# Batched matmul on one core: the first loads take their runs in another order over the partitions

One Trainium2 chip, one core. The metric is the time of one execution on the device in microseconds, as the median of several runs.

## The reference

```python
def setup_inputs():
    batch, m, k, n = 16, 512, 512, 512
    # a: [batch, k, m] float32, b: [batch, k, n] float32, normal random numbers

def reference(a, b):
    return np.matmul(a.transpose(0, 2, 1), b).astype(np.float32)
```

Sixteen products of 512 x 512 matrices. A and B are 16.8 MB each, the output is 16.8 MB: 50.33 MB go through the DMA engines, as q1 counts them.

## The kernel before

The first two batches are loaded one by one, with four rows of 512 numbers (8 KB) per partition, so that the first matmuls can start when one batch of A and B has landed. All later batches are loaded in pairs, with 16 KB per partition. Which row of k sits in which partition doesn't matter to the result, as long as A and B agree, because the contraction sums over all of them.

```python
P = 128; RV = 4; R = 8                      # the program derives these
# run p (rows 4p .. 4p+3, 8 KB) goes to partition p
in0_v = [x.rearrange("batch (p r) m -> batch p r m", r=RV) for x in (a, b)]
...
for j in range(2):                          # j = 0 is A, j = 1 is B
    nc.sync.dma_start(x_ts[j][:, 0:RV, :], in0_v[j][0]).then_inc(s_f[j], 16)    # batch 0
for j in range(2):
    nc.sync.dma_start(x_ts[j][:, RV:R, :], in0_v[j][1]).then_inc(s_x[j], 16)    # batch 1
for n in range(2, 2 * pairs):               # pairs of batches, 2 MB each
    if n >= NX:
        nc.sync.wait_ge(s_in, n - NX + 1)   # until a buffer has been cast
    ...
# VectorE casts a landed tile to bf16, TensorE multiplies, ScalarE copies PSUM out;
# SP issues seven outputs once the last input's first half is in, and the eighth at the end
```

Of the kernel before, what the change touches and what calls it, by code (L numbers as in the profile page):

```python
# [8 lines left out]
def kernel(  # L9
# [6 lines left out]
    nc = tc.nc  # L16
    P = 128
    batch, K, M = a.shape
# [9 lines left out]
    R = K // Q  # L28
    V = 2
    RV = R // V  # L30
# [3 lines left out]
    in_v = [x.rearrange("(pair g) (q r) m -> pair (g q) r m", g=G, r=R) for x in (a, b)]  # L34


    in0_v = [x.rearrange("batch (p r) m -> batch p r m", r=RV) for x in (a, b)]
    out_v = out.rearrange("(pair g) (c t) n -> pair c g t n", g=G, t=T)

    NX = 4  # L40
# [10 lines left out]
    x_ts = [pool.tile([P, R, M], f32, name=f"x{j}") for j in range(NX)]  # L51
# [5 lines left out]
    s_x = [tc.alloc_semaphore(f"s_x{j}") for j in range(NX)]  # L57
    s_f = [tc.alloc_semaphore(f"s_f{j}") for j in range(2)]
# [9 lines left out]

    with tc.tile_critical(no_gpsimd_drain=True):  # L69
        for j in range(2):  # L70
            nc.sync.dma_start(x_ts[j][:, 0:RV, :], in0_v[j][0]).then_inc(s_f[j], 16)
        for j in range(2):
            nc.sync.dma_start(x_ts[j][:, RV:R, :], in0_v[j][1]).then_inc(s_x[j], 16)
        for n in range(2, 2 * pairs):
            if n >= NX:
                nc.sync.wait_ge(s_in, n - NX + 1)
            src, x = in_v[n % 2][n // 2], x_ts[n % NX]
# [141 lines left out]
```

## Time and profile before

| | before |
|---|---|
| time, median of the first 3 runs | 123.24 us (123.08 to 123.38) |
| span of the profiled run | 121.7 us |
| DMA engines' share of the span | 97.8% |
| busiest compute engine | TensorE, 53% |
| first DMA issued, first packet, first cast | 0.94 us, 1.96 us, 5.81 us |

The table of stretches that the prediction shows says the rest: half rate for the first 1.3 us of transfers, then a steady 430 GB/s to the end.

### The profile page before, as it was taken

How to read it: one execution, taken by the hardware profiler on the slowest of the kernel's cores; microseconds unless marked ns; L12 is line 12 of the kernel's file. 1: busy time of each engine (PE TensorE's matmuls, PEld its weight loads, DVE VectorE, ACT ScalarE, POOL GpSimd, SP SyncE). 2: the span in 40 equal slices, each digit the busy share in tenths (PEclk: the TensorE clock that was granted, in tenths of full speed). 3: DMA queues.
4: the chain of work that ended last, by engine and by line, in shares of the span. 5: the costliest groups of instructions: out<-in, count | busy, mean ns of one | idle time of the engine just before them, and what ended most of it. 6: DMA issues, size and time to landing. Idle time of an engine off the chain costs nothing. (4 is left out here: it accounts for less than half of the span.)

```text
span 121.7 us, 1207 instructions
## 1 busy us (share of the span) xinstructions
PE 65.0 (53%) x480; PEld 35.6 (29%) x480; DVE 38.0 (31%) x48; ACT 32.2 (26%) x41; POOL 0.2 (0%) x4
## 2 busy tenths in 40 slices
PE   0007937919989759739969919999930000000000
PEld 0002302306646336414536605556610000000000
DVE  0051061095684094082464446266000000000000
ACT  4000330330390840840191480065190000000000
POOL 0000000000000000000000000000000000000000
PEclk9999996799999999976999996899999555555555
DMA  3999999999999999999999999999999999999993
GB/s 59 428 428 426 463 431 431 431 431 436 431 431 431 431 431 431 431 431 431 431 431 431 431 431 399 431 420 423 426 428 423 428 431 431 431 431 428 431 428 162
DMA packets 4912, 50.33 MB, mean 414 GB/s; under 512 B 432, under 2 KB 432, under 8 KB 432
## 3 DMA queue, kind: packets, MB, share of 16 engines
q1 hardware_dynamic: 4912, 50.33, 97.8%
HBM read 33.55 MB, written 16.78 MB: 414 GB/s over the span
## 5 line engine op out<-in xcount | busy, mean ns | idle before, releaser
L151 PE MATMUL ps<-bbf,abf 64*128 64x512 bf16 x448 | 53.1, 394 | 11.9 <-PEq L146 11.9
L151 PEld LDWEIGHTS ps<-bbf,abf 64*128 64x128 bf16 x448 | 31.4, 113 | 33.7 <-issue 19.2
L176 ACT COPY o<-ps 128x1024 f32<-128x1024 f32 x28 | 26.3, 1026 | 39.3 <-PE ps L151 39.3
L113 DVE CAST abf<-x 128x2048 bf16<-128x2048 f32 x14 | 17.2, 1225 | 20.6 <-PE ps L151 14.9
L113 DVE CAST bbf<-x 128x2048 bf16<-128x2048 f32 x14 | 17.1, 1224 | 11.8 <-DMA x<-in_b_dram 11.8
L131 PE MATMUL ps<-bbf,abf 128*128 128x512 bf16 x32 | 11.9, 554 | 12.5 <-PEq L129 12.5
L131 PEld LDWEIGHTS ps<-bbf,abf 128*128 128x128 bf16 x32 | 4.3, 138 | 19.6 <-issue 19.1
L170 ACT COPY o<-ps 128x1024 f32<-128x1024 f32 x4 | 4.1, 1014 | 19.2 <-PE ps L131 19.2
L94 DVE CAST abf<-x 128x2048 bf16<-128x2048 f32 x2 | 2.5, 1228 | 12.7 <-PE ps L131 6.9
L94 DVE CAST bbf<-x 128x2048 bf16<-128x2048 f32 x2 | 2.5, 1226 | 1.2 <-DMA x<-in_b_dram 1.2
L181 ACT ACTIVATE done<-done 1x1 uint32<-1x1 uint32 x8 | 1.6, 197 | 0.0
L170 ACT ACT_TABLE_LOAD x1 | 1.3, 1283 | 0.9 <-SPq L69 0.9
L119 DVE MEMSET done<- 1x1 f32 x14 | 0.8, 59 | 0.0
L98 DVE MEMSET done<- 1x1 f32 x2 | 0.1, 59 | 0.0
L203 POOL MEMSET const-uint8-127<- 128x1 uint8 x1 | 0.1, 103 | 0.0
L203 POOL MEMSET const-bfloat16-1.0<- 128x1 bf16 x1 | 0.1, 102 | 0.0
L203 POOL MEMSET const-float32-0.0<- 128x1 f32 x1 | 0.1, 99 | 0.2 <-issue 0.2
L203 POOL MEMSET const-float32-1.0<- 128x1 f32 x1 | 0.1, 99 | 0.0
## 6 DMA issues: line engine op xcount, KB each, us to landing
out_dram<-o SPq DMA_DIRECT2D x8, 2048.0 KB, 22.2
x<-in_a_dram SPq DMA_DIRECT2D x7, 2048.0 KB, 12.1
x<-in_b_dram SPq DMA_DIRECT2D x6, 2048.0 KB, 15.6
x<-in_b_dram SPq DMA_DIRECT2D x4, 1024.0 KB, 12.1
x<-in_a_dram SPq DMA_DIRECT2D x2, 1024.0 KB, 6.8
```

The lines of the kernel that those rows point to most:

```text
L94: nc.vector.tensor_copy(out=bf_ts[0][:], in_=x_ts[j][:, u * RV:(u + 1) * RV, :]).then_inc(s_cast, 1)
L98: nc.vector.memset(dve_done[:, j:j + 1], 0.0).then_inc(s_in, 1)
L113: nc.vector.tensor_copy(out=(bbf_ts if n % 2 else abf_ts)[v][:], in_=x_ts[n % NX][:, v * RV:(v + 1) * RV, :],).then_inc(s_cast, 1)
L119: nc.vector.memset(dve_done[:, n:n + 1], 0.0).then_inc(s_in, 1)
L131: mm = nc.tensor.matmul(ps_ts[0][h][:, t % 2, :], a_m[:, r, t], bbf_ts[0][:, r, :], start=(r == 0), stop=(r == RV - 1),)
L151: mm = nc.tensor.matmul(ps_ts[g][h][:, t % 2, :], a_m[:, t], bbf_ts[v][rows, r, :], start=(v == 0 and r == 0), stop=(v == V - 1 and r == R ...
L170: nc.scalar.copy(out=o_ts[0][:, g, 2 * h:2 * h + 2, :], in_=ps_ts[0][h][:]).then_inc(s_ev[h], 1)
L176: ev = nc.scalar.copy(out=o_ts[i % NO][:, g, 2 * h:2 * h + 2, :], in_=ps_ts[g][h][:])
L181: nc.scalar.memzero(act_done[:, i:i + 1]).then_inc(s_out, 1)
L203: nc = _bacc.Bacc("TRN2", target_bir_lowering=False, num_devices=1)
```

## The change

Its intent: partitions 0, 4, 8 and so on are to read neighbouring 8 KB runs of DRAM rather than runs 32 KB apart. Partition 4s+i now takes run 32i+s, for A and B alike. "Starts" are below the first addresses that partitions 4s ask for: 32 KB apart before, 8 KB apart after, and 64 KB apart in the later loads of 16 KB per partition. "Hops" are the distances from one partition to the next within such a group of four: 8 KB before, 256 KB after. Both are read from the program.

```diff
-    in0_v = [x.rearrange("batch (p r) m -> batch p r m", r=RV) for x in (a, b)]
+    in0_v = [x.rearrange("batch (i s r) m -> batch s i (r m)", i=4, r=RV) for x in (a, b)]
...
-            nc.sync.dma_start(x_ts[j][:, 0:RV, :], in0_v[j][0]).then_inc(s_f[j], 16)
+            nc.sync.dma_start(x_ts[j][:, 0:RV, :].rearrange("p r m -> p (r m)"), in0_v[j][0]).then_inc(s_f[j], 16)
...
-            nc.sync.dma_start(x_ts[j][:, RV:R, :], in0_v[j][1]).then_inc(s_x[j], 16)
+            nc.sync.dma_start(x_ts[j][:, RV:R, :].rearrange("p r m -> p (r m)"), in0_v[j][1]).then_inc(s_x[j], 16)
```

The source has three dimensions now (32, 4, 2048).

## The prediction

No trace shows which engine takes which run, and a rival rested on it, in which the first 4 MB would take up to twice as long (an assumption: 133 us, chance 0.03; that was the whole chance given to slower by over 2%). The sum: +0.02 us for the issue, -0.25 us for the first packet and 0 for the rest, in all -0.23 us, so 123.0 us. The 9.8 us in the rival on hops is 4.19 MB at the 430 GB/s of the stretches.

> **What bounds the kernel now.** I read the page's summary first, then its DMA rows, then the chain of waits, then a table of stretches of time that I cut by hand, and last the single DMA packets of the trace.
>
> ```profile
> span 121.7 us, 1207 instructions
> PE 65.0 (53%) x480; PEld 35.6 (29%) x480; DVE 38.0 (31%) x48; ACT 32.2 (26%) x41; POOL 0.2 (0%) x4
> DMA  3999999999999999999999999999999999999993
> GB/s 59 428 428 426 463 431 431 431 431 436 431 431 431 431 431 431 431 431 431 431 431 431 431 431 399 431 420 423 426 428 423 428 431 431 431 431 428 431 428 162
> q1 hardware_dynamic: 4912, 50.33, 97.8%
> ```
>
> No compute engine is busy for more than 53% of the span; the 16 DMA engines are busy for 97.8% of it, and the bytes per slice stand at about 430 GB/s from the second slice to the last but one. So the span is 50.33 MB at that rate (50.33 MB / 430 GB/s = 117.0 us) plus what happens before the stream is at its rate and after its last byte: 121.7 - 117.0 = 4.7 us. Only the first slice is weak (59 GB/s), and the last (162 GB/s). The chain of waits agrees in its own way: it holds compute of a total of 8% of the span and ends when the eighth output was issued at 91.7 us; everything after that is data draining.
>
> The next table cuts the span where the single packets change their behaviour. The last three columns are the granted TensorE clock, the DMA engines' mean busy share and what they moved.
>
> ```profile
> 0.00:1.95 1.95, 0.00 (x0) 0.00 (x0) 0.00 (x0) 1.05 (x1) 0.20 (x4) 1.00 0.00 0
> 1.95:3.25 1.30, 0.00 (x0) 0.00 (x0) 0.00 (x0) 0.23 (x1) 0.00 (x0) 1.00 1.05 214
> 3.25:4.25 1.00, 0.00 (x0) 0.00 (x0) 0.00 (x0) 0.00 (x0) 0.00 (x0) 1.00 1.02 426
> 4.25:18.45 14.20, 6.57 (x16) 2.26 (x16) 4.51 (x5) 2.03 (x2) 0.00 (x0) 1.00 1.01 430
> 18.45:64.20 45.75, 36.24 (x281) 20.15 (x283) 22.90 (x31) 17.27 (x23) 0.00 (x0) 0.93 1.01 432
> 64.20:91.60 27.40, 22.21 (x186) 13.22 (x182) 10.57 (x14) 11.58 (x17) 0.00 (x0) 0.94 1.00 426
> 91.60:119.40 27.80, 0.00 (x0) 0.00 (x0) 0.00 (x0) 0.00 (x0) 0.00 (x0) 0.55 1.01 427
> ```
>
> Three things are to be seen. Nothing moves for 1.95 us: launch, and the first DMA's issue. Then for 1.30 us the engines count as fully busy and yet move 214 GB/s, half the rate. From 3.25 us on the rate is 426 to 432 GB/s whatever is moved: the two first batches in 8 KB runs (to 18.45 us), later inputs in 16 KB runs, outputs in 8 KB runs.
>
> The packets explain the 1.30 us. The median 8 KB packet takes 309 ns (8192 B / 309 ns x 16 = 424 GB/s), the 16 KB one 611 ns. The first packet of each of the 16 streams is different. Eight streams start at 1.96 to 2.04 us and their first packet takes 1.12 to 1.29 us; the other eight start at 2.12 to 2.21 us and take 0.79 to 0.87 us. Every second packet is back at 309 ns. The 16 KB loads and the later 8 KB packets show nothing of the kind, except for one or two packets per stream at 314 to 328 ns near 4.1 us. I chained the packets to streams by their ends (the trace doesn't name the engine). A stream's time over 309 ns per packet is 0.87 to 1.0 us in the slow eight and 0.50 to 0.57 us in the fast eight, nearly all of it the first packet; one stream also loses 0.25 us to slightly slow packets at 84 to 90 us, and it ends last, at 120.34 us. The streams have no gaps, so what is lost at the start is still there at the end: the slow eight end at 120.0 to 120.1 us, the fast at 119.75 to 119.9 us.
>
> [...]
>
> **The change part by part.** It removes no byte, no DMA, no wait and no instruction. The four DMAs of 1 MB each keep 128 runs of 8 KB and their destination. Only which run goes where moves: partition 4s+i gets run 32i+s. A and B change alike, so the contraction, which sums over all 128 partitions, is the same sum in another order: casts (1.23 us each, 4 in this part) and matmuls (32 of them) cost the same. In order of time:
> 1. Issue. The first DMA's issue takes 392 ns, the second 422 ns, with the plain two-dimensional source; a later partial load, whose source is strided, takes 433 ns. A third source dimension may cost a like amount: an estimate of 0 to 0.04 us on the path for the first DMA, nothing for the other three, which are issued while data flows.
> 2. First packet. [...] If all of the first packet's excess came from the spread of the starts, the slow eight would gain 1.23 - 0.31 = 0.92 us. If the slow eight merely came to the 0.80 us of the fast eight, they would gain about 0.4 us, and the stream that ends last, one of the slow eight at its start, would end at about 119.9 us. If the excess is just the wait for the first data of an idle memory system, nothing is gained. I take 0.92 us at a chance of 0.1, 0.4 us at 0.4, nothing at 0.5: 0.25 us.
> 3. The rest of the 4 MB. [...] The streams are held at 309 ns by something that 64 KB starts, 32 KB starts, reads and writes share, so I expect no loss: 0 us.
> 4. From there on all is shifted. Compute has slack: the first cast starts when A has landed (5.81 us), and DMA issues that wait for a cast are ahead of need, as the missing gaps show. A gain at the start should arrive whole at the end.
> Sum: +0.02 - 0.25 = -0.23 us, so 123.24 - 0.23 = 123.0 us.
>
> **The rivals.** *Start latency only.* The excess belongs to the first access, whatever the address; the time stays at 123.2 us. For it: B's first packets, at the same 32 KB spread, cost no more than 20 ns extra, and so do the other new tensors' regions. Against it: two groups of eight with different excess, where the group that starts later is done earlier.
> [...]
> *Hops cost rate.* 256 KB hops over a region of 1 MB slow the first 4 MB by a few per cent: 5% of 9.8 us is 0.5 us, 123.7 us. Against it: the constant 309 ns. I give it 0.08.
> *All of it.* The full 0.92 us is gained: 122.3 us.
>
> **How range and chances follow.** Predicted 123.0 us. The three times of before spread over 0.3 us, and another chip may add a like amount. The low end takes the 0.92 us case less some of that noise, 122.4 us; the high end takes no gain and 0.2 us of noise, 123.45 us. A change of 2% is 2.46 us, more than twice the 0.92 us that the first packets hold, so faster by over 2% has only 0.01; [...] within 2% 0.96.
>
> **What would show it.** Right: the same stretch from about 1.95 to 3.25 us with more than 214 GB/s, the slow eight first packets near 0.8 us, 309 ns for the rest to 18 us, A landing earlier than 5.8 us and the last output by as much. Wrong in step 2: first packets as before and the span within 0.1 us. Wrong in step 3: 8 KB packets over 309 ns before 18 us, or under 420 GB/s there. Wrong in step 4: first packets faster, yet the last stream ends at 120.3 us; then something later absorbs the gain, such as the slow packets near 84 to 90 us.

## More of the kernel before

The timeline of the kernel before adds how the first loads are issued. Columns: start in us, duration in us, engine, line, operation, tiles, count; SPq is the queue of the engine that issues DMAs.

```profile
0.94 0.39 SPq L71 DMA_DIRECT2D x<-in_a_dram  x1
1.39 0.42 SPq L71 DMA_DIRECT2D x<-in_b_dram  x1
1.86 0.42 SPq L73 DMA_DIRECT2D x<-in_a_dram  x1
2.33 0.65 SPq L73 DMA_DIRECT2D x<-in_b_dram  x1
5.81 1.23 DVE L94 CAST abf<-x 128x2048 bf16<-128x2048 f32 x1 [5.81 <-DMA x<-in_a_dram]
```

The first three issues take 0.39 to 0.42 us each, the fourth 0.65 us. The first packet moves 0.63 us after the first issue ends, and the first cast waits until the whole first tile of A has landed.

## The result, and the profile after

The changed kernel takes 123.45 us (median of 6 runs, 123.40 to 123.95), beside 123.26 us (6 runs, 123.08 to 123.38) for the kernel before: a ratio of 1.0022, with a 95% interval of 1.0004 to 1.0039. Ratios here are the mean time of one kernel's fast runs over that of the other's of the same rounds, so not quite the ratio of the medians. The small difference is a loss, where the prediction had a gain of 0.23 us.

The summary and DMA rows of the changed kernel, for those that the prediction shows:

```profile
span 121.7 us, 1207 instructions
PE 61.7 (51%) x480; PEld 34.8 (29%) x480; DVE 38.1 (31%) x48; ACT 32.2 (26%) x41; POOL 0.2 (0%) x4
DMA  1999999999999999999999999999999999999994
GB/s 51 409 423 420 447 431 436 436 431 436 436 431 431 436 431 436 431 436 431 431 431 431 431 431 398 431 425 420 423 428 425 431 425 428 431 431 431 431 428 183
q1 hardware_dynamic: 4912, 50.33, 97.3%
```

The bound is the same. The DMA share has lost half a point, and the first slices moved less (51 and 409 GB/s, before 59 and 428). Five of the seven stretches of before (length, busy time of the engines, granted clock, DMA share, GB/s):

```profile
0.00:1.95 1.95, 0.00 (x0) 0.00 (x0) 0.00 (x0) 1.05 (x1) 0.20 (x4) 1.00 0.00 0
1.95:3.25 1.30, 0.00 (x0) 0.00 (x0) 0.00 (x0) 0.23 (x1) 0.00 (x0) 1.00 0.46 158
3.25:4.25 1.00, 0.00 (x0) 0.00 (x0) 0.00 (x0) 0.00 (x0) 0.00 (x0) 1.00 1.08 442
4.25:18.45 14.20, 5.68 (x19) 2.37 (x20) 4.83 (x6) 2.03 (x2) 0.00 (x0) 1.00 1.02 432
91.60:119.40 27.80, 0.00 (x0) 0.00 (x0) 0.00 (x0) 0.00 (x0) 0.00 (x0) 0.50 1.01 428
```

The busy share of the second stretch fell from 1.05 to 0.46: the first packets start later and are short. But the bytes fell too, from 214 to 158 GB/s (the view counts a packet in the stretch in which it starts). Later stretches are as before (432 against 430 GB/s up to 18.45 us), so the 256 KB hops cost no steady rate. The timeline of the changed kernel shows where the start went:

```profile
0.95 0.64 SPq L72 DMA_DIRECT2D x<-in_a_dram  x1
1.65 0.58 SPq L72 DMA_DIRECT2D x<-in_b_dram  x1
2.27 0.60 SPq L74 DMA_DIRECT2D x<-in_a_dram  x1
2.91 0.70 SPq L74 DMA_DIRECT2D x<-in_b_dram  x1
6.13 1.23 DVE L95 CAST abf<-x 128x2048 bf16<-128x2048 f32 x1 [6.13 <-DMA x<-in_a_dram]
```

The first three issues take 0.58 to 0.64 us instead of 0.39 to 0.42; the fourth, which took 0.65 us before, takes 0.70. Nothing hides the first one: it ends 0.25 us later, at 1.59 us. The first packet starts 0.49 us later, at 2.45 us, and the first cast 0.32 us later.

In the single packets, the first packet of a stream took 0.34 to 0.58 us in this trace (0.54 to 0.89 us in the two taken later), against 0.79 to 1.29 us in the first trace of before. Read alone, that looks like the hoped-for gain. The experiments show that this reading is wrong.

### The profile page after: what moved, and what is told of

It reads as the page before. It is cut to its first block, busy times and chain, and to the rows that moved or that the text cites. A ratio compares the mean times of both kernels' runs of the same rounds, so it can differ in the third digit from the quotient of the medians.

```text
span 121.7 us, 1207 instructions
## 1 busy us (share of the span) xinstructions
PE 61.7 (51%) x480; PEld 34.8 (29%) x480; DVE 38.1 (31%) x48; ACT 32.2 (26%) x41; POOL 0.2 (0%) x4
## 2 busy tenths in 40 slices
DMA packets 4913, 50.33 MB, mean 413 GB/s; under 512 B 433, under 2 KB 433, under 8 KB 433
## 3 DMA queue, kind: packets, MB, share of 16 engines
q1 hardware_dynamic: 4912, 50.33, 97.3%
## 4 chain that ended last, share of the span: by engine, by line
DMA 59%; DVE 6%; issue 3%; ACT 3%; SPq 3%; ACTq 0%
DMA x<-in_b_dram 53%; DMA out_dram<-o 6%; ACT o L177 3%; DVE bbf L114 3%; DVE abf L114 3%; SPq L74 1%; SPq L72 1%; SPq L80 0%; DVE done L120 0%; ACTq L70 0%; SPq L215 0%; SPq L70 0%
## 5 line engine op out<-in xcount | busy, mean ns | idle before, releaser
L132 PE MATMUL ps<-bbf,abf 128*128 128x512 bf16 x32 | 8.7, 435 | 12.8 <-PEq L130 12.8
L132 PEld LDWEIGHTS ps<-bbf,abf 128*128 128x128 bf16 x32 | 3.7, 122 | 17.3 <-issue 15.1
```

The costliest lines, as they stand in the source:

```text
L132: mm = nc.tensor.matmul(ps_ts[0][h][:, t % 2, :], a_m[:, r, t], bbf_ts[0][:, r, :], start=(r == 0), stop=(r == RV - 1),)
```

## The experiments

Two measures are used, both worked out from the trace's single DMA packets. The **lag** of a stream (one of the 16) is the time at which its first 64 KB have landed, less eight packets at the steady 306 ns; 64 KB is its share of A's first tile. The streams have almost no gaps and equal bytes (3.14 to 3.15 MB each in the first trace of both kernels), so a lag at the start should still be there at the end; the check below the table tests this. The **start delay at 0.25 MB (or 3 MB)** is the time at which that many bytes have landed over all streams, less the time they take at the steady rate (16 x 8192 B in 305.9 ns); smaller is better. Addresses, and so the distances of starts, are those that the kernel asks for: which engine takes which run no trace shows. Streams are chained by the ends of their packets, which works for 8 KB and 16 KB packets and not well for mixes with smaller ones; for those only the second measure is used. A trace is one execution.

```
kernel               first issue   mean lag           latest stream's lag  first cast at      (us, one number per trace)
before               0.39          2.82 2.77 2.81     2.98 2.93 3.01       5.81 5.77 5.83
changed              0.64          3.03 2.97 2.95     3.35 3.31 3.28       6.13 6.06 6.11
e1 / rev_same_chip   0.64          3.16 3.13          3.41 3.24            6.24 6.07
e2_pitch_2k          0.39          2.71               3.19                 6.01
e3_late_start        0.39, 0.54 later  3.30           3.57                 6.39
e4_second_batch      0.39          2.87               3.01                 5.83
e5_first_batch       0.64          3.00               3.32                 6.14
e6_pitch_16k         0.39          2.86               3.32                 6.12
```

The first cast follows the latest stream and not the mean: cast less latest lag is 2.83 us before, 2.78 us after, 2.80 us in e6, 2.82 us in e2.

Chaining can mistake a packet for another stream's. The trace also holds 16 completion events of each DMA, which need no chaining; their mean for A's first tile, less eight packets, is the mean lag plus 0.32 to 0.35 us in every trace of the table. They exist for every DMA, so they can be followed to the last store:

```
                                A's first tile: mean, last event         last store: mean, last event       (us, one pair per trace)
before                          5.60, 5.79   5.56, 5.75   5.60, 5.80     120.30, 120.71   120.26, 120.58   120.30, 120.48
changed                         5.81, 6.10   5.74, 6.04   5.73, 6.08     120.53, 120.78   120.52, 120.84   120.50, 120.77
e1 / rev_same_chip              5.94, 6.21   5.92, 6.05                  120.64, 120.88   120.62, 120.73
e2_pitch_2k                     5.49, 5.98                               120.22, 120.67
e6_pitch_16k                    5.64, 6.10                               120.37, 120.79
```

The mean lag lasts: with the old addresses in the new form it is 0.34 us above before at A's tile and 0.34 us at the end, in the changed kernel 0.17 and 0.23 us. The last event's need not: e2's is 0.21 us late at A's tile and within the range of before at the end.

**1. The form of the DMA with the old addresses.** Each group of four runs is taken in reverse. The source has three dimensions as in the change, starts are still 32 KB apart, and the result is correct. The runs of a group now descend in address; what that does by itself was not tested.

```diff
+    rev_v = [[bass.AP(tensor=x.tensor, offset=x.offset + q * K * M + 3 * RV * M,
+                      ap=[[4 * RV * M, P // 4], [-RV * M, 4], [1, RV * M]]) for q in range(2)] for x in (a, b)]
-            nc.sync.dma_start(x_ts[j][:, 0:RV, :], in0_v[j][0])...
+            nc.sync.dma_start(x_ts[j][:, 0:RV, :].rearrange("p r m -> p (r m)"), rev_v[j][0])...   # and batch 1 alike
```

> Source of three dimensions as in the change, but the first runs 32 KB apart as before: each group of four runs is only taken in reverse (correct result). Theory ISSUE (the three-dimensional source makes each issue some 0.25 us longer and the first packets start about 0.5 us later; the neighbouring starts take back about as much from the first packets): first issue about 0.64 us, first packets start at 2.45 us and still take 0.8 to 1.2 us, first cast at about 6.4 us, time 123.26 + 0.5 to 0.7 = 123.8 to 124.0 us. Rival FIXED (data can't arrive before about 3 us whatever is asked when, and the long first packets are only waiting): first packets short (0.3 to 0.6 us), first cast at 6.1 us, time as the changed kernel, 123.45 us.

Measured: 123.57 us (5 runs), ratio 1.0031 (1.0017 to 1.0045). The view of its first DMA line gives the issue durations (ns, minimum/median/maximum):

```profile
L73 SPq DMA_DIRECT2D x<-in_a_dram x1: 637/637/637, 0.9 to 0.9; - x1
L73 SPq DMA_DIRECT2D x<-in_b_dram x1: 578/578/578, 1.6 to 1.6; - x1
```

The same 637 and 578 ns as in the changed kernel, with other addresses: the long issue belongs to the form of the source and not to its addresses. The loss is 0.33 us, where 0.5 to 0.7 us had been expected, so the theory was right in kind and too large in size; I had added the whole 0.49 us by which the first packets start later. First packets took 0.31 to 1.04 us, neither all short nor all long as either theory had said.

**2. Neighbouring starts with the cheap issue, by overlapping runs.** The result is wrong on purpose: at a pitch of 2 KB starts are 8 KB apart.

```diff
+    nar_v = [[bass.AP(tensor=x.tensor, offset=x.offset + q * K * M,
+                      ap=[[M, P], [1, RV * M]]) for q in range(2)] for x in (a, b)]   # pitch 2 KB, runs of 8 KB
# the four first loads read nar_v[j][0] and nar_v[j][1]
```

> Wrong result on purpose: the plain two-dimensional source, 8 KB runs that overlap at a pitch of 2 KB, [...]. Theory ISSUE: issue 0.39 us, first packets start at 1.96 us and take 0.35 to 0.6 us, first cast at 5.1 to 5.4 us, time 122.6 to 122.9 us. Rival FIXED: first packets start at 1.96 us and still end at 2.9 to 3.2 us, so they take 0.8 to 1.2 us; first cast 5.8 us, time 123.2 us. Since bytes are read four times over, a rate above the steady 430 GB/s would speak for a memory-side limit; neither theory expects it.

Measured: 123.23 us, ratio 0.9995 (0.9982 to 1.0009). The first 0.25 MB have a start delay of 2.72 us (before: 2.96, 2.87, 2.91), but packets of up to 0.50 us follow at 3.0 to 3.5 us, and of up to 0.57 us where B begins. The mean lag gains 0.09 us on the mean of before (2.80 us), and the latest stream loses 0.22 us. The expected gain of 0.4 to 0.6 us didn't come. The first cast is later than before (6.01 against 5.77 to 5.83 us) and yet the time is the same: a late stream at A's tile does not by itself make the kernel longer. What the fourfold reading of the same bytes adds can't be told apart here.

**3. The start made later.** The first DMA waits for a memset on VectorE.

```diff
+        nc.vector.memset(late[:], 0.0).then_inc(s_late, 1)      # late: 1 x 384
+        nc.sync.wait_ge(s_late, 1)
         for j in range(2):
             nc.sync.dma_start(x_ts[j][:, 0:RV, :], in0_v[j][0])...
```

> The kernel before, with its first DMA made to wait for a memset of 384 columns on VectorE, so that it is issued 0.4 to 0.6 us later. Theory ISSUE: everything shifts by that delay, first packets still take 0.8 to 1.2 us, time 123.7 to 123.9 us. Rival FIXED: first packets shorten by the delay and the time stays within 0.1 us of before.

Measured: 124.05 us, ratio 1.0071 (1.0057 to 1.0085). Its timeline:

```profile
1.08 0.38 DVE L72 MEMSET late<- 1x384 f32 x1 [1.08 <-SPq L71]
1.48 0.39 SPq L75 DMA_DIRECT2D x<-in_a_dram  x1
6.39 1.23 DVE L98 CAST abf<-x 128x2048 bf16<-128x2048 f32 x1 [4.93 <-DMA x<-in_a_dram]
```

The issue is 0.54 us later, the first cast 0.58 us later than at 5.81 us, the mean lag 0.50 us above 2.80 us. So data doesn't wait for a fixed moment: FIXED falls, and a delay of the first issue reaches the data in full. The time rose by 0.81 us, more than the delay; in this trace the span goes on for 1.52 us after the last packet against 1.31 us before, so some 0.2 us of it is not the start. What in the edit adds that tail wasn't looked into.

**4. Only the second batch in the new order.**

```diff
-            nc.sync.dma_start(x_ts[j][:, RV:R, :], in0_v[j][1])...
+            nc.sync.dma_start(x_ts[j][:, RV:R, :].rearrange("p r m -> p (r m)"), perm_v[j][1])...   # perm_v: the change's view
```

> Only the second batch's two DMAs take the new order; the first two stay as before. Theory ISSUE: longer issues are hidden behind flowing data, first packets as before, time 123.26 within 0.1 us. Rival HOPS [...]: half of the change's loss stays, some 0.1 us, and 8 KB packets over 309 ns appear between 8 and 12 us.

Measured: 123.23 us, ratio 0.9997 (0.9983 to 1.0010). The views of its two DMA lines, first batch and second:

```profile
L72 SPq DMA_DIRECT2D x<-in_a_dram x1: 393/393/393, 0.9 to 0.9; - x1
L74 SPq DMA_DIRECT2D x<-in_a_dram x1: 625/625/625, 1.9 to 1.9; - x1
L74 SPq DMA_DIRECT2D x<-in_b_dram x1: 639/639/639, 2.5 to 2.5; - x1
```

Two issues of 0.63 us are in it (in the kernel before these two took 0.42 and 0.65 us) and cost nothing; data of the first two DMAs flows meanwhile. HOPS, that the 256 KB hops cost rate, falls too: no loss. And one more thing: the first DMA is that of the kernel before, yet its streams' first packets start anywhere from 2.00 to 2.84 us and take 0.31 to 1.13 us, where before they started at 1.96 to 2.21 us and took 0.79 to 1.29 us. They end at 3.06 to 3.31 us, before at 2.91 to 3.27 us. So a first packet's start moves from run to run far more than its end, and its length alone is no measure of a loss.

**5. Only the first batch in the new order.** The counterpart of 4, with the edit on the other pair of lines.

> Only the first batch's two DMAs take the new order. Theory ISSUE, as the first four runs left it (the first DMA's longer issue costs about 0.3 us; neighbouring starts win about 0.26 us on the first 0.25 MB and some 0.2 us of it is lost again before 3 MB): all of the change's effect lies in the first batch, so time 123.4 to 123.5 us, first cast at 6.1 us. If the second batch carries part of the loss (a third and fourth long issue that starve the streams), the time is nearer to 123.3 us.

Measured: 123.50 us (6 runs, one at 123.91), ratio 1.0018 (1.0006 to 1.0030), first cast at 6.14 us, latest lag 3.32 us: with run 4 this says that the changed kernel's whole effect lies here. The profiled run was the one at 123.91 us; it lost another 0.4 us later in the stream, which is not part of the comparison.

**6. Starts twice as far apart, cheap issue.** Wrong result: the pitch is 16 KB, so that starts are 64 KB apart (`ap=[[R * M, P], [1, RV * M]]`).

> Wrong result on purpose: plain two-dimensional source with the cheap issue, 8 KB runs at a pitch of 16 KB, [...] twice as far as before. If the distance of the starts is what delays the first bytes, the first 0.25 MB come later than before by 0.1 to 0.3 us and the time is 123.3 to 123.5 us; if only neighbouring starts differ from all the others, the time is 123.25 us within 0.1.

Measured: 123.63 us, ratio 1.0030 (1.0018 to 1.0043). The start delay at 0.25 MB is 2.97 us, as before (2.87 to 2.96 us); the mean lag is up 0.06 us, but three streams have packets of 1.27 to 1.40 us, and the latest lag is 3.32 us, 0.35 us up. The time, 0.41 us up, lies above both expected ranges, so neither expectation was right. It fits the latest stream better than the mean, where e2 fits the mean better; which of the two sets the time isn't settled. What this run does show is that addresses alone, with the cheap issue, can cost 0.4 us.

**7 and 8. Neighbouring starts with cheap issues and without overlap.** Two candidates, both correct: A and B of the first batch in a piece of 2 KB runs and one of 6 KB runs (starts 8 KB apart on the first piece), or in two halves of 4 KB runs (16 KB apart).

```diff
+    lead_v = [x[0, 0:P, :].rearrange("(p r) m -> p r m", r=1) for x in (a, b)]
+    rest_v = [x[0, P:K, :].rearrange("(p r) m -> p r m", r=RV - 1) for x in (a, b)]
+            nc.sync.dma_start(x_ts[j][:, 0:1, :], lead_v[j]).then_inc(s_f[j], 16)
+            nc.sync.dma_start(x_ts[j][:, 1:RV, :], rest_v[j]).then_inc(s_f[j], 16)
# the other:
+    half_v = [[x[0, q * K // 2:(q + 1) * K // 2, :].rearrange("(p r) m -> p r m", r=RV // 2) for q in range(2)] for x in (a, b)]
```

> Candidate, correct result: the first batch's tile is loaded as a piece of 128 runs of 2 KB ([...] no overlap, cheap issue), then one of 128 runs of 6 KB. Two more DMAs in all. Theory ISSUE: first issue 0.39 us, the first bytes earlier by about 0.25 us, time 122.9 to 123.1 us, unless the early win is lost again as it was in the changed kernel, then 123.2 us. Against it: the small first piece (0.26 MB, 0.6 us of data) may run dry before the second is under way, which would cost up to 0.2 us.

Measured: 124.24 us (123.60 to 124.88), ratio 1.0086 (1.0052 to 1.0119). The start delay at 0.25 MB was 2.30 us, 0.6 us better than before, but at 0.5 MB 2.90 us: the first sixteen 6 KB packets took 0.33 to 0.93 us, and by 3 MB (3.08 us) all was given back. The six runs fall in two groups, 123.60 to 123.79 us and 124.69 to 124.88 us; the trace is of the first group, so where the second loses a further 1.1 us isn't known.

> Candidate, correct result: the first batch's tile is loaded in two halves of 128 runs of 4 KB each, [...]. Theory ISSUE: half of the way to neighbouring starts, time 123.0 to 123.2 us; if distance doesn't matter, 123.25 us.

Measured: 124.10 us (123.12 to 124.49), ratio 1.0071 (1.0054 to 1.0088). One of six runs, the profiled one, took 123.12 us; the others 123.81 us and more. Neither candidate beats the kernel before.

**9 to 12. Second traces.** The kernel before twice more, the changed kernel and the candidate in halves once more, one look each.

> The kernel before, once more, for a second trace. A stream's lag is the time at which its first 64 KB have landed, less 8 packets at the steady 306 ns. In the first trace the 16 streams' lags are 2.82 us in the mean and 2.98 us for the latest. If lag is set by issue and addresses and not by chance, the mean is again 2.7 to 2.9 us and the latest 2.9 to 3.1 us; the single first packets may differ freely, as they did in the run with only the second batch changed.

> The kernel before, a third trace, as a measure of what one trace of the start can show: mean lag 2.7 to 2.9 us, latest 2.9 to 3.1 us, and time within 0.15 us of 123.24 us.

> The changed kernel, once more. First trace: mean lag 3.03 us, latest stream 3.35 us. Theory LATEST STREAM (all streams carry equal bytes without gaps, so the latest stream at the start sets the end): mean 2.95 to 3.1 us, latest 3.25 to 3.45 us, 0.3 us later than before. If the latest stream is as early as in the kernel before (3.0 us), then the spread was chance and the cause of the longer time is open.

> The candidate in two halves of 4 KB runs, once more, to see where its slow runs (123.8 to 124.5 us) lose against its one fast run (123.1 us). Theory LATEST STREAM: in a slow run one or some streams fall behind by 0.7 to 1.2 us in the first megabyte and end that much after the others; the mean of the streams is as early as in the fast run. Rival: all streams are late alike, or the loss lies in the outputs after 79 us.

The kernel before took 123.27 and 123.17 us, the changed one 123.53 us. Lags are in the table: before, the mean is 2.77 to 2.82 us and the latest 2.93 to 3.01 us; changed, 2.95 to 3.03 and 3.28 to 3.35 us, and the ranges don't touch. First packets of the kernel before differ here too: in one trace eight streams start at 2.61 to 2.70 us and take 0.31 to 0.45 us, in the other two streams take 0.34 us and their second packets 0.92 and 1.05 us. The long packet is not even always the first.

The candidate in halves took 124.16 us this time. Its stretches show the loss:

```profile
2.95:3.45 0.50, 0.00 (x0) 0.00 (x0) 0.00 (x0) 0.00 (x0) 0.00 (x0) 1.00 0.99 393
3.95:4.45 0.50, 0.00 (x0) 0.00 (x0) 0.00 (x0) 0.00 (x0) 0.00 (x0) 1.00 1.06 426
4.45:4.95 0.50, 0.00 (x0) 0.00 (x0) 0.00 (x0) 0.00 (x0) 0.00 (x0) 1.00 1.09 262
4.95:5.45 0.50, 0.00 (x0) 0.00 (x0) 0.00 (x0) 0.00 (x0) 0.00 (x0) 1.00 0.93 188
```

It runs at full rate early and then falls to 188 to 262 GB/s around 5 us, at the packets of B's halves. The start delay goes from 2.54 us at 1 MB to 3.39 us at 2 MB. That is not what the theory LATEST STREAM had said (some streams late, the mean early); the mean itself is late, as its rival had it, though at the start and not in the outputs.

**13 to 15. Addresses or packet size?** The pieces again, with the old addresses (starts 32 KB apart): A and B in halves, A alone in halves, A alone in 2 KB and 6 KB.

```diff
+            for r in (slice(0, 2), slice(2, RV)):
+                nc.sync.dma_start(x_ts[j][:, r, :], in0_v[j][0][:, r, :]).then_inc(s_f[j], 16)
```

> Correct result. A and B of the first batch in two DMAs of 4 KB runs each, [...] same DMAs and packet sizes as the candidate with 16 KB starts. If addresses made that candidate's first bytes early, the first 0.25 MB are back at the kernel before (2.87 to 2.96 us, against 2.37 to 2.56). If packet size did, they stay at 2.4 to 2.6 us. Time: if 16 KB starts made the candidate's stalls, 123.0 to 123.3 us; if its small packets or extra DMAs did, 123.8 to 124.5 us again.

> Correct result. Only A's first tile is split in two halves of 4 KB runs, addresses as before, B as before. If packet size makes first bytes early and B's split the stalls: first 0.25 MB at 2.4 to 2.6 us and time 122.8 to 123.1 us, a version faster than both kernels. If the one-off stall of the start comes anyway, only later, time 123.2 to 123.5 us.

> Correct result. A's first tile as a piece of 2 KB runs and one of 6 KB runs, addresses as before, B as before. Same two outcomes as for the halves of A: 122.8 to 123.1 us, or 123.2 to 123.6 us with a stall of 0.5 us or more at the 6 KB packets.

Measured: 124.48 us (ratio 1.0100, 1.0086 to 1.0115), 124.00 us (1.0057, 1.0044 to 1.0070) and 123.85 us (six runs, two at 124.82 and 125.05; 1.0081, 1.0047 to 1.0115). All lose, so the slow halves came from splitting the first tile and not from the 16 KB starts. Smaller packets and more DMAs to issue came together here and weren't taken apart. The start delays, in us:

```
                                starts apart    at 0.25 MB    at 3 MB
before (three traces)           32 KB           2.87 to 2.96  2.95 to 3.00
A, B: 2 KB then 6 KB            8 KB            2.30          3.08
A:    2 KB then 6 KB            32 KB           2.96          3.39
A, B: halves of 4 KB            16 KB           2.56, 2.37    2.90, 3.50
A, B: halves of 4 KB            32 KB           2.73          3.65
A:    halves of 4 KB            32 KB           2.69          3.47
```

At like packet sizes nearer starts do bring the first quarter megabyte earlier, by 0.17 to 0.66 us (the 2 KB pair differs in B's split as well). Against the kernel before, every one of them but the candidate's one fast run is behind by 3 MB. At like packet sizes the nearer starts are still ahead there (3.08 against 3.39 us; 2.90 and 3.50 against 3.65 us), in single traces of different chips, so it is the splitting that costs, and nearer starts soften it. In these traces the stall moves; it is not removed. In the kernel with A alone in halves it lies at 2.45 to 3.95 us:

```profile
2.45:2.95 0.50, 0.00 (x0) 0.00 (x0) 0.00 (x0) 0.00 (x0) 0.00 (x0) 1.00 0.83 279
2.95:3.45 0.50, 0.00 (x0) 0.00 (x0) 0.00 (x0) 0.00 (x0) 0.00 (x0) 1.00 0.91 254
3.45:3.95 0.50, 0.00 (x0) 0.00 (x0) 0.00 (x0) 0.00 (x0) 0.00 (x0) 1.00 0.93 205
```

**16 and 17. The changed kernel and its form with old addresses on one chip.**

> The changed kernel on the same chip as the next. Time 123.4 to 123.5 us; first 64 KB of the streams at a mean lag of 2.95 to 3.05 us, the latest at 3.25 to 3.4 us.

> The three-dimensional source with 32 KB starts, again. If neighbouring starts take back some 0.1 us: 123.5 to 123.65 us, mean lag 3.1 to 3.2 us. If they take back nothing, the two times agree within 0.05 us, and the whole loss of the change is its issue.

Measured: 123.50 us (1.0024, 1.0010 to 1.0037) and 123.61 us (1.0030, 1.0016 to 1.0044). The medians of the two differ by 0.11 us, their means by 0.06. The stretch 1.95 to 3.25 us holds the two effects. Kernel before (second trace, another chip), changed kernel (this run), old addresses in the new form (this run), one fence each:

```profile
1.95:3.25 1.30, 0.00 (x0) 0.00 (x0) 0.00 (x0) 0.23 (x1) 0.00 (x0) 1.00 0.81 202
```

```profile
1.95:3.25 1.30, 0.00 (x0) 0.00 (x0) 0.00 (x0) 0.23 (x1) 0.00 (x0) 1.00 0.73 183
```

```profile
1.95:3.25 1.30, 0.00 (x0) 0.00 (x0) 0.00 (x0) 0.23 (x1) 0.00 (x0) 1.00 0.55 113
```

The form alone takes 202 to 113 GB/s: 89 x 1.30 us / 430 = 0.27 us of full rate. The addresses give back 70 x 1.30 / 430 = 0.21 us of it in this stretch. Over all traces the stretch has 202 to 214 GB/s before, 158 to 183 changed, 113 and 120 in the form with old addresses; the means make it 0.27 and 0.17 us.

## Why the prediction was wrong

The bound and the class were right: the time is the stream of 50.33 MB, and the change moves it by far less than 2%. The direction was wrong, because one term was too small by far and another too large.

- **Step 1, the issue. Predicted 0 to 0.04 us; measured 0.25 us in the issue itself and about 0.34 us in all. This is the step that failed.** The first issue went from 392 to 637 ns. With the old addresses the new form has a mean lag 0.34 us above before (3.14 against 2.80 us), and a time 0.33 us and 0.38 us above the same rounds' medians. Run 3 shows that a delay of the first issue reaches the data in full, so 0.25 of the 0.34 us is accounted for; the other 0.09 us comes between the issue's end and the landing, and its cause is open. The row from which the step was read, a strided partial load at 433 ns, was no likeness: its twin, equally strided, took 328 ns like the whole loads, and in both, source and destination are split as 128 rows, while here 32 x 4 on one side meets 128 on the other. Three dimensions alone aren't it either: the output stores have 128 x 2 x 2048 on both sides, and the fastest of seven was issued in 403 ns (the median took 1262 ns, for a reason that wasn't looked into):

```profile
L87 SPq DMA_DIRECT2D out_dram<-o x7: 403/1262/4927, 78.8 to 84.8; - x7
```

Why this form takes longer to issue is not shown. That the form of the source carries the cost, without the change's addresses, is shown by runs 1 and 17; that the second batch's long issues cost nothing, by run 4. The two DMAs of the first batch weren't taken apart.
- **Step 2, the first packet. Predicted -0.25 us, measured about -0.1 us, which the intervals don't separate from nothing.** Addresses were compared at one form on one chip: 123.50 against 123.61 us (the descending order of that form may be part of the difference). In the traces the mean lag gains 0.16 us (2.98 against 3.14 us, means of three and two traces), but the latest stream nothing (3.31 against 3.33 us). By the completion events the last of A's tile comes 0.05 us earlier (6.07 against 6.13 us in the mean). So the gain falls mostly to streams that aren't last; the spread from the first to the last event of A's tile was 0.31 to 0.39 us before and is 0.42 to 0.55 us in the changed kernel. The reading behind the step failed as well: I took a first packet's length over 309 ns for time lost to its address. Runs 4, 9 and 10 show that length and start trade against each other with little change in the end, and that the two groups of eight, which the prediction held against its rival, are not in every trace. By the prediction's own signs the result (first packets shorter, yet the end later) would have been laid to step 4; the runs with one thing changed lay it to step 1.
- **Step 3, the hops. Predicted 0.** Right for the steady stream: 432 GB/s to 18.45 us and no loss in run 4. Not quite in the first batch: the start delay of the changed kernel worsens from 0.25 MB to 3 MB by 0.07 to 0.24 us (before: 0.04 to 0.09 us). So part of what near starts win at first is lost again. The completion events say the same: against the old addresses in the new form, the changed kernel is 0.17 us ahead in the mean at A's tile and about 0.11 us at the last store. Why is open.
- **Step 4, the shift arrives whole. Nearly right.** At the end of the stream the last packet but one stream's lands at 120.33 to 120.42 us in three traces of the changed kernel, at 120.05 to 120.11 us in three of before: +0.27 us. The very last is +0.22 us (120.45 against 120.23 us in the mean), as one stream loses some 0.3 us to slightly slow packets near 84 to 92 us in every trace, and before it is this one that ends last. That hides a little of the later start. The mean of the last store's events is 0.23 us later than before, with 0.17 us at A's tile.
- **The rivals.** "Start latency only" came nearest, since near starts gained only about 0.1 us, but put the time at 123.2 us, as it shared the small issue; that the distance of the starts never matters isn't shown, and run 6 speaks against it. "All of it" (122.3 us) fell with the gain. The rival above (133 us) is refuted by the time and by the 8 KB packets: 97% of them lie within 4 ns of 309 ns in the changed kernel. The long issue as a loss appears among the rivals nowhere; it stood in the sum with about a tenth of its size. That the measured 123.45 us still touches the upper end of the predicted range is luck: that end was made of no gain and 0.2 us of noise, not of a loss.

Put together from the measured terms: +0.34 us for the form, less 0.16 us in the mean or about nothing in the latest stream, gives +0.18 to +0.34 us for the start; the kernel measured +0.19 and +0.27 us. The low end is by construction the changed kernel's own mean lag (2.98 less 2.80 us), so this checks only that the lag reaches the time, and not the two terms apart.

What stays open: what the one-off stall of 0.5 to 1 us in the first 2 to 4 MB is, which every traced version pays somewhere (first packets, second packets, the 6 KB pieces, or B's halves), why 64 KB starts cost 0.41 us, and why splitting the first tile makes it dearer (0.6 to 1.2 us in all).

## What to carry to other kernels

Before an address pattern is changed for the memory's sake, compare how long its DMA takes to issue: a source whose outer dimension no longer matched the destination's made the first issue 0.25 us longer here. Behind flowing data that cost nothing (run 4: two issues of 0.63 us, 123.23 us); at the first DMA of the program it was paid in full (run 1: 0.33 us more time). A packet's duration in a trace is no loss by itself (run 4: first packets of 0.31 to 1.13 us, no loss in time); compare when equal bytes have landed, in the mean and in the latest of the streams: the first cast waits for the latest, but the whole time need not follow it (run 2). Make the first load in one piece with the plainest pattern; finer first pieces brought the first bytes 0.2 to 0.6 us earlier and the end 0.6 to 1.2 us later.
